# A two-layer transformer trunk: VectorE operands moved to PSUM, modulation products placed one by one, QKV weight splits on GpSimd

## Chip, cores and metric

One core of one Trainium2 chip. The metric is the device time of one execution in microseconds; the runs shown are medians of several executions.

## What is computed

1024 latent tokens and 256 context tokens of width 1024 pass two layers. Cut to what matters here:

```python
for i in range(DEPTH):
    ...
    hx = _modulate(_rms(x, norm_mix_g[i]), sx1, cx1)
    if i % 2 == 0:
        x = x + gx1 * _conv_fourier_mixer(hx, ab_w_in[j], ab_conv_w[j], ab_w_out[j])
        ...
    else:
        w = na_w_qkv[j]
        hc = _modulate(_rms(ctx, norm_mix_g[i]), sc1, cc1)
        q = _heads(hx, w[:, :hd], na_q_g[j])
        k = _heads(hx, w[:, hd:2 * hd], na_k_g[j])
        v = _heads(hx, w[:, 2 * hd:])
        ...
    x = x + gx2 * _mlp(_modulate(_rms(x, norm_mlp_g[i]), sx2, cx2), mlp_w1[i], mlp_w2[i])
    if not last:
        ctx = ctx + gc2 * _mlp(_modulate(_rms(ctx, norm_mlp_g[i]), sc2, cc2), mlp_w1[i], mlp_w2[i])
return x

def _mlp(h, w1, w2):
    return jnp.square(jax.nn.relu(h @ w1)) @ w2
```

The modulation (shift, scale and gate of each sublayer) is `cond_x @ ada_w[i] + ada_b[i]` for latent and the same with `cond_c` for context tokens.

Everything is fp32 accurate. The kernel gets there by splitting each operand into a rounded high part (fp32r) and a low part, low = value - high, and adding three matmuls: high x high, high x low, low x high.

## The kernel before, in words

Tokens lie in three chunks of columns: 0 and 1 with 512 latent tokens each, 2 with 256 context tokens. `xT[d][ci]` is the residual stream, 8 row tiles `d`. A bank is one of eight PSUM tiles of 128x512 (`bank()`); `tmp()` has four and `keep()` three SBUF tiles of that size. A weight tile is 128x512, two lie in a raw tile; raw tiles rotate through three buffers (tag `wraw`), split tiles through four (`wsp`). `split_act` (L251) makes a split: ScalarE (ACT) casts the high part (L252), the named engine subtracts for the low part (L253).

The program's stages: mixer of layer 0 (to 425 us), the context pass (425 to 664), the first MLP for latent tokens (664 to 1343), QKV (1343 to 1712), attention, second MLP.

**Context pass** (from L1268). The MLP of layer 0 on the 256 context tokens: 128 weight tiles, each with twelve matmuls of 128x256 (L299 to L301). `ctx_make` (L952) splits them, every third on VectorE (DVE), the others on GpSimd (POOL). In the up half, `dense` fills a bank; ACT takes ReLU and squares it twice, once as fp32r high part, and DVE subtracts (L1275 to L1278). In the down half `residual` (L316) adds the bank to `xT`. After each group `beside_step` runs one step of a list `beside0`: the norm that feeds the latent MLP (`Norm.stat` and `Norm.out`, chunks 1 and 0; odd row tiles multiply on POOL at L412, even ones on DVE at L405), then the token sums `sums_12` and `sum_3` (`whole` at L985 joins high and low part of a quarter, differences follow, `parts_of` splits them), and `sum_4`.

**First MLP** (`Seven`, L1013). Products of quarters are combined by sums, seven instead of eight, in 16 units. In a unit `head` and `tail` make the up half: sums from PSUM with `s1` (L1119, L1123, L1010), then `squared`; `down` makes 16 groups with a residual add each. Beside `down` run the products of the modulation for layer 1: `ada_step` (L216) takes one raw tile of `ada_w` and does eight multiply-and-accumulate operations (L223) in one go, twice per unit in units 0 to 13. The last unit's `down_by_chunk` has the squares (`Norm.square`, L378) and statistics (L388, a matmul with ones) of layer 1's first norm beside it.

**QKV** (from L1457): six units of 512 columns, each with 8 or 10 token tiles of 24 matmuls (L1466 to L1468). The norm's remaining outputs stand in the first unit (`later`); `load_qkv` splits four of the next unit's tiles early and four after its last tile; `tick` runs what was put off: transposes of normalised queries and keys (`turn`, L102) two or four tiles later, and `ada_filler`, eight products at a time.

Order of work: PE's instructions keep the program's order where `in_order` says so (L1168); everywhere else the scheduler orders each engine's queue by a simulated timeline when the program is built. SP issues the DMAs in its own order.

## Time and profile before

| | us |
|---|---|
| median of 3 runs | 2775.05 (2773.75 to 2775.78) |
| the profiled execution | 2776.96 |
| its span, first to last instruction | 2775.0 |
| TensorE (PE) busy | 2624.0 |
| VectorE (DVE) busy | 1952.0 |
| ScalarE (ACT) busy | 1041.8 |
| GpSimd (POOL) busy | 1236.3 |

Mean granted clock of TensorE 0.976. Busy time counts a matmul longer at the lower clock, so a stage's loss is idle time and clock together.

### The profile page before, as it was taken

To read this page: it belongs to the slowest core of one execution; us is meant where nothing else is said; L and a number is where in the kernel's file an instruction comes from. 1 tells how busy PE (TensorE), PEld (TensorE's weight loads), DVE (VectorE), ACT (ScalarE), POOL (GpSimd) and SP (SyncE) were. 2 spreads that over 40 slices of the span, in tenths; PEclk is the share of its full clock that TensorE was granted. 3 is DMA by queue.
4 is the path that set the end of the run, shared out by engine and by line. 5 is a ranking of instruction groups with operands and counts; after the bars stand their busy time and mean duration, and the time that the engine had idled before them with its cause. 6 is when DMAs were issued, how large, how long until landed. Compare 5 with 4: busy or idle time off the path is not lost. (4 is left out here: it accounts for less than half of the span.)

```text
span 2775.0 us, 38416 instructions
## 1 busy us (share of the span) xinstructions
PE 2624.0 (95%) x13883; PEld 2179.2 (79%) x13883; DVE 1952.0 (70%) x3986; ACT 1041.8 (38%) x2232; POOL 1236.3 (45%) x975
## 2 busy tenths in 40 slices
PE   7999898798999999999789999899999899999999
PEld 5888778797888888888667787688877688888887
DVE  5797679955776777775987453887879856556555
ACT  4211246554223223223432233666654323322322
POOL 3332347777445445445410011444447744544543
PEclk9999899999999999999999999899999999999999
DMA  7244324353222222222256344343411111111112
GB/s 249 67 139 130 119 62 129 111 171 122 84 73 88 82 71 84 82 74 77 80 167 184 117 131 152 115 152 107 139 50 39 42 43 61 54 49 50 61 46 84
DMA packets 170530, 273.08 MB, mean 98 GB/s; under 512 B 11308, under 2 KB 110924, under 8 KB 170084
## 3 DMA queue, kind: packets, MB, share of 16 engines
q1 hardware_dynamic: 168900, 268.01, 30.4%
q8 instruction: 109, 1.79, 0.3%
q10 hardware_dynamic: 1440, 2.62, 0.2%
q14 instruction: 81, 0.66, 0.1%
HBM read 241.21 MB, written 29.37 MB: 98 GB/s over the span
## 5 line engine op out<-in xcount | busy, mean ns | idle before, releaser
L253 POOL TENSOR_TENSOR wsp<-raw,wsp 128x512 fp32r<-128x512 f32 x454 | 644.3, 1424 | 782.7 <-ACT wsp L252 761.3
L316 DVE SCALAR_TENSOR_TENSOR xT<-ps,mods,xT 128x512 f32<-128x512 f32 (+1 forms) x672 | 470.5, 715 | 149.7 <-PE ps L301 148.9
L252 ACT CAST wsp<-raw 128x512 fp32r<-128x512 f32 x510 | 311.8, 618 | 648.2 <-PE ps L301 321.0
L223 DVE CUSTOM_DVE_ANT_0 junk<-raw,cond_b 128x256 bf16<-128x256 f32 x640 | 351.7, 550 | 106.2 <-DMA raw<-in_ada_t_dram 75.6
L1103 PE MATMUL ps<-mh,wsp 128*128 128x512 f32 (+1 forms) x1216 | 349.6, 368 | 8.1 <-DVE ny L1119 6.3
L1103 PEld LDWEIGHTS ps<-mh,wsp 128*128 128x128 f32 x1216 | 215.8, 189 | 49.3 <-ACT tmp L1003 4.4
L299 PE MATMUL ps<-uh,wsp 128*128 128x512 f32 x528 | 208.2, 394 | 8.8 <-DVE xT L316 6.7
L1103 PE MATMUL ps<-ml,wsp 128*128 128x512 f32 (+1 forms) x608 | 213.1, 368 | 0.0
L300 PE MATMUL ps<-ul,wsp 128*128 128x512 f32 x528 | 206.7, 391 | 1.2 <-DVE ul L1006 1.2
L301 PE MATMUL ps<-uh,wsp 128*128 128x512 f32 x528 | 206.6, 391 | 0.0
L301 PE MATMUL ps<-w,wsp 128*128 128x256 f32 (+1 forms) x512 | 172.4, 345 | 10.8 <-DVE wsp L253 8.6
L253 POOL TENSOR_TENSOR wsp<-tmp,wsp 128x512 fp32r<-128x512 f32 x60 | 81.4, 1356 | 224.5 <-ACT wsp L252 224.5
L300 PE MATMUL ps<-w,wsp 128*128 128x256 f32 (+1 forms) x512 | 173.6, 342 | 4.6 <-DVE w L1278 4.6
L299 PE MATMUL ps<-w,wsp 128*128 128x256 f32 (+1 forms) x512 | 173.1, 345 | 4.3 <-ACT wsp L252 3.0
L1010 DVE TENSOR_TENSOR tmp<-ps,ny 128x512 f32<-128x512 f32 x90 | 62.2, 691 | 126.4 <-PE ps L1103 124.4
L1005 POOL TENSOR_TENSOR tmp<-tmp 128x512 f32<-128x512 f32 x128 | 141.2, 1104 | 8.7 <-ACT uh L1004 6.7
L252 ACT CAST wsp<-tmp 128x512 fp32r<-128x512 f32 x60 | 37.3, 622 | 262.3 <-PE ps L301 257.6
L299 PE MATMUL ps<-hh,wsp 128*128 128x512 f32 (+1 forms) x360 | 130.4, 362 | 4.3 <-ACT wsp L252 3.9
L300 PE MATMUL ps<-hl,wsp 128*128 128x512 f32 (+1 forms) x360 | 129.5, 360 | 2.0 <-DVE hl L413 1.4
L301 PE MATMUL ps<-hh,wsp 128*128 128x512 f32 (+1 forms) x360 | 128.3, 357 | 1.5 <-POOL wsp L253 1.5
L299 PEld LDWEIGHTS ps<-uh,wsp 128*128 128x128 f32 x528 | 99.8, 189 | 35.8 <-DVE xT L316 7.3
L1103 PEld LDWEIGHTS ps<-ml,wsp 128*128 128x128 f32 x608 | 110.3, 189 | 17.8
(374 smaller groups left out, 6529.5 us busy)
## 6 DMA issues: line engine op xcount, KB each, us to landing
raw<-in_mlp_w_dram SPq DMA_DIRECT2D x192, 512.0 KB, 3.5
raw<-in_ada_t_dram SPq DMA_DIRECT2D x80, 512.0 KB, 3.5
...
```

Source lines behind the costliest of these rows:

```text
L223: DVE.tensor_tensor_reduce(out=junk, in0=raw[:, d * 256:d * 256 + 256], in1=cond_b, op0=ALU.mult, op1=ALU.add, scale=1.0, scalar=0.0, accu ...
L252: ACT.copy(dst_hi, src)
L253: lo_eng.tensor_tensor(out=dst_lo, in0=src, in1=dst_hi.bitcast(F32), op=ALU.subtract)
L299: PE.matmul(ps, lhsT=whi, rhs=ahi, start=first, stop=False)
L300: PE.matmul(ps, lhsT=whi, rhs=alo, start=False, stop=False)
L301: PE.matmul(ps, lhsT=wlo, rhs=ahi, start=False, stop=last)
L316: DVE.scalar_tensor_tensor(out=xT[dt][ci], in0=ps, scalar=mods[l][:, 24 * k + 16 + dt, s:s + 1], in1=xT[dt][ci], op0=ALU.mult, op1=ALU.add)
L1005: POOL.tensor_tensor(out=r, in0=r, in1=r, op=ALU.mult)
L1010: DVE.tensor_tensor(out=c, in0=ps, in1=s, op=ALU.add)
L1103: PE.matmul(ps[:, cs], lhsT=a, rhs=p, start=(first and kt == 0 and n == 0), stop=(kt == 3 and n == 2), skip_group_check=True)
```

## The change

What it does:

- The modulation products come one at a time (`ada_op`). In the first MLP two loads and two products per place in units 0 to 5, one of each in units 6 to 14; in QKV five products per token tile, in every tile from the second unit on and from the sixth tile of the first. Altogether 168 products are ordered into the first MLP (224 before) and 216 behind it (160 before).
- A `Norm` with `psum=(0, 1)` keeps its statistic `y` and each product `a` of chunks 0 and 1 in PSUM banks, and all its outputs go DVE, ACT, DVE. Both the context pass's norm and layer 1's first norm have it.
- `ctx_make`: every fourth weight tile is split by ACT, then ACT copies the high part to a bank and DVE subtracts from there; the other three go to POOL.
- Token sums: one `whole` on POOL, then `minus` twice on DVE into a bank.
- Context ReLU: DVE squares in the bank (max with 0, times r) in place of ACT.
- Last unit of the first MLP: the context squares stand in its tail, the context statistic right behind it.
- QKV: all splits on POOL.
- Second MLP: `sum_3` and `sum_4` in the new form, spread over two stages of eight places.

The diff, cut to what is spoken of:

```diff
--- before.py
+++ after.py
@@ -213,26 +213,38 @@
-    def ada_step():
...
-        l, m, kq, dh, raw = ada_raw.pop(0)
-        for s in range(2):
-            cond_b = ada_cond(kq, s)
-            for d in range(4):
-                DVE.tensor_tensor_reduce(out=junk, in0=raw[:, d * 256:d * 256 + 256], in1=cond_b, op0=ALU.mult,
-                                         op1=ALU.add, scale=1.0, scalar=0.0, accum_out=parts[:, kq, 4 * dh + d, s:s + 1])
...
+    def ada_op():
...
+        (l, m, kq, dh, raw), s, d = ada_open.pop(0)
+        cond_b = ada_cond(kq, s)
+        DVE.tensor_tensor_reduce(out=junk, in0=raw[:, d * 256:d * 256 + 256], in1=cond_b, op0=ALU.mult,
+                                 op1=ALU.add, scale=1.0, scalar=0.0, accum_out=parts[:, kq, 4 * dh + d, s:s + 1])
...
+    def ada_step():
+        for _ in range(8):
+            ada_op()
@@ -386,6 +402,13 @@
+            if ci in self.psum:
+                y, y0, t = bank()[:, :w], tmp()[:, :w], tmp()[:, :w]
+                self.y[ci] = y
+                return [lambda: ACT.activation(y0, ps[:, :w], AF.Abs_reciprocal_sqrt, scale=1.0 / D, bias=eps),
+                        lambda: DVE.scalar_tensor_tensor(out=t, in0=y0, scalar=-0.5 / D, in1=y0, op0=ALU.mult, op1=ALU.mult),
+                        lambda: DVE.scalar_tensor_tensor(out=t, in0=ps[:, :w], scalar=D * EPS, in1=t, op0=ALU.add, op1=ALU.mult),
+                        lambda: DVE.scalar_tensor_tensor(out=y, in0=t, scalar=1.5, in1=y0, op0=ALU.add, op1=ALU.mult)]
@@ -398,10 +421,10 @@
-            x, y, a = xT[dt][ci], self.y[ci], tmp()[:, :w]
+            x, y, a = xT[dt][ci], self.y[ci], (bank if ci in self.psum else tmp)()[:, :w]
-            if dt % 2 == 0 if on_dve is None else on_dve:
+            if ci in self.psum or (dt % 2 == 0 if on_dve is None else on_dve):
                 return (lambda: DVE.scalar_tensor_tensor(out=a, in0=x, scalar=g, in1=y, op0=ALU.mult, op1=ALU.mult),
...
@@ -857,7 +880,7 @@
-    norm = Norm(0, 1, m_hi, m_lo)
+    norm = Norm(0, 1, m_hi, m_lo, psum=(0, 1))
@@ -955,7 +978,14 @@
             w = wp.tile([P, 1024], F32R, tag="wsp", name="wsp")
-            split_act(w[:, 0:512], w[:, 512:1024], w_raw[n][:, 512 * k:512 * k + 512], DVE if w_at[0] % 3 == 1 else POOL)
+            raw = w_raw[n][:, 512 * k:512 * k + 512]
+            if w_at[0] % 4 == 1:
+                p = bank()
+                ACT.copy(w[:, 0:512], raw)
+                ACT.copy(p, w[:, 0:512].bitcast(F32))
+                DVE.tensor_tensor(out=w[:, 512:1024], in0=raw, in1=p, op=ALU.subtract)
+            else:
+                split_act(w[:, 0:512], w[:, 512:1024], raw, POOL)
@@ -1110,21 +1140,28 @@
             self.product(b, self.t["t2"], True)
+            step()
             DVE.tensor_tensor(out=u2, in0=b, in1=s1, op=ALU.add)
             self.product(a, self.quarter(upper, H0), False)
+            step()
             squared(tmp(), *part(0, H0), a)
             self.product(b, self.quarter(lower, H1), False)
...
             DVE.tensor_tensor(out=u3, in0=b, in1=s1, op=ALU.add)
             self.product(c, self.t["t1"], True)
+            step()
             c22 = added(c, u3)
             squared(c22, *part(1, H1), c22)
             self.product(b, self.t["t4"], False)
+            step()
...
@@ -1179,27 +1216,49 @@
+        def minus(self, p, b, t):
+
+            DVE.tensor_tensor(out=p, in0=b[0].bitcast(F32), in1=t, op=ALU.subtract)
+            DVE.tensor_tensor(out=p, in0=p, in1=b[1].bitcast(F32), op=ALU.add)
...
             def first():
-                f[0], f[1] = room(), room()
+                f[0] = room()
                 whole(b11, POOL, f[0])
-                whole(b12, DVE, f[1])
             def second():
-                f[2] = room()
-                whole(b22, POOL, f[2])
-                parts_of(t1, f[0], DVE)
+                f[1] = bank()
+                self.minus(f[1], b12, f[0])
 
             def third():
-                DVE.tensor_tensor(out=f[2], in0=f[2], in1=f[0], op=ALU.subtract)
+                parts_of(t1, f[1], DVE)
+
+            def fourth():
+                f[2] = bank()
+                ACT.copy(f[0], f[1])
+                self.minus(f[2], b22, f[0])
+
+            def fifth():
+                parts_of(t2, f[2], DVE)
                 self.t.setdefault("t1", []).append(t1)
                 self.t.setdefault("t2", []).append(t2)
 
-            return [first, lambda: DVE.tensor_tensor(out=f[0], in0=f[1], in1=f[0], op=ALU.subtract), second, third,
-                    lambda: parts_of(t2, f[2], DVE)]
+            return [first, second, third, fourth, fifth]
         def sum_3(self, kt, room=tmp):
...
+                f[0] = room()
+                whole(b12, POOL, f[0])
+
+            def second():
+                f[1] = bank()
+                self.minus(f[1], b22, f[0])
+
+            return [first, second, lambda: parts_of(b12, f[1], DVE)]
...
+            f2, p = room(), bank()
+            whole(self.t["t2"][kt], POOL, f2)
+            self.minus(p, self.quarter([kt + 4], H0)[0], f2)
+            parts_of(t4, p, DVE)
@@ -1230,10 +1291,12 @@
+        if (ci, which) == (2, 0):
+            return big("acc", F32)
...
-    norm1 = Norm(1, 0, a_hi, a_lo, room1)
+    norm1 = Norm(1, 0, a_hi, a_lo, room1, psum=(0, 1))
@@ -1270,11 +1333,10 @@
-            t = tmp()
-            r, q = t[:, 0:w2], t[:, w2:2 * w2]
-            ACT.activation(r, ps[:, :w2], AF.Relu)
+            r, q = tmp()[:, 0:w2], ps[:, :w2]
+            ACT.activation(r, q, AF.Relu)
             ACT.activation(uh[f][:, F0], r, AF.Square)
-            ACT.activation(q, r, AF.Square)
+            DVE.scalar_tensor_tensor(out=q, in0=q, scalar=0.0, in1=r, op0=ALU.max, op1=ALU.mult)
             DVE.tensor_tensor(out=ul[f][:, F0], in0=q, in1=uh[f][:, F0].bitcast(F32), op=ALU.subtract)
@@ -1305,8 +1367,14 @@
     def between0(i, us):
-        steps = [lambda: None] * 4 + [ada_issue, lambda: (ada_step(), ada_issue()), lambda: None, ada_step]
-        s0.down(us, None, steps if i < 14 else ())
+        def ada(n):
+            if ada_raw:
+                for _ in range(n):
+                    ada_op()
+
+        two = i < 6
+        s0.down(us, (lambda m, ci: (ada_issue() if (m, ci) == (4, 0) or two and (m, ci) == (4, 1) else None,
+                                    ada(2 if two else 1) if m > 3 and (m, ci) > (4, 0) else None)) if i < 15 else None)
@@ -1316,14 +1384,26 @@
-        todo = [[lambda d=d: norm1.square(d, 2) for d in range(4 * k, 4 * k + 4)] for k in range(2)]
-        todo += [[], [], [lambda: norm1.stat(2)]] + [[lambda d=d: norm1.out(d, 2, True) for d in (2 * k, 2 * k + 1)] for k in range(4)]
-        todo += [[], [], [], [], [lambda: norm1.stat(0)]] + [[lambda d=d: norm1.out(d, 0)] for d in range(2)]
-        s0.down_by_chunk(us, lambda m, ci: norm1.square(m, ci, POOL if m % 2 else DVE), todo)
-
+        norm1.stat(2)
+        todo = [[lambda d=d: norm1.out(d, 2, True) for d in (2 * k, 2 * k + 1)] for k in range(4)]
+        todo += [[] for _ in range(7)] + [[lambda: norm1.stat(0)]] + [[lambda d=d: norm1.out(d, 0)] for d in range(4)]
+        s0.down_by_chunk(us, lambda m, ci: norm1.square(m, ci, POOL if m % 2 and ci else DVE), todo)
+    s0.beside = [lambda: None] * 3 + [lambda k=k: [norm1.square(d, 2) for d in range(4 * k, 4 * k + 4)] for k in range(2)]
...
-    fillers.extend([ada_filler] * 21)
+    def ada_ops(n):
+        def run():
+            if not ada_raw and ada_next:
+                ada_issue()
+            if len(ada_raw) == 1 and ada_next:
+                ada_issue()
+            for _ in range(n):
+                ada_op()
+        return run
+
+    fillers.extend([ada_ops(5)] * (-(-8 * len(ada_next + ada_raw) // 5) + 1))
@@ -1338,7 +1418,7 @@
-            split_act(wt[:, 0:512], wt[:, 512:1024], raw, POOL if kt % 2 else DVE)
+            split_act(wt[:, 0:512], wt[:, 512:1024], raw, POOL)
@@ -1451,7 +1531,7 @@
-    later = {0: outs(0, 2, 5), 1: outs(0, 5, 8), 3: [lambda: norm1.stat(1)] + outs(1, 0, 2), 4: outs(1, 2, 5), 5: outs(1, 5, 8)}
+    later = {0: outs(0, 4, 6), 1: outs(0, 6, 8), 2: [lambda: norm1.stat(1)] + outs(1, 0, 1), 3: outs(1, 1, 3), 4: outs(1, 3, 5), 5: outs(1, 5, 8)}
@@ -1469,7 +1549,7 @@
-            tick(n == 2 or n < 5 and i > 3 and i % 2 == 0 or 0 < n < 5 and i % 2 == 0)
+            tick(n > 0 or i > 4)
@@ -1500,7 +1580,7 @@
-            qn = keep()
+            qn = x_all[2][:, 2 * (0, 2, 3)[i]:2 * (0, 2, 3)[i] + 2, :].rearrange("p a b -> p (a b)") if n == 0 and i < 3 else keep()
@@ -1516,7 +1596,7 @@
-            after(4 if n == 0 and i < 4 else 2, turn)
+            after(4 if n == 0 and i < 3 else 2, turn)
@@ -1685,8 +1765,7 @@
-        for f in s1.sums_12(kt, *(halves(op_.tile([P, NLAT], F32R, tag=g, name=g)) for g in ("oh", "ol"))):
-            f()
+        s1.sums_12_plain(kt, *(halves(op_.tile([P, NLAT], F32R, tag=g, name=g)) for g in ("oh", "ol")))
@@ -1712,8 +1791,9 @@
-    s1.down(us[:2], None, [lambda kt=kt: [f() for f in s1.sum_3(kt)] for kt in range(4)])
-    s1.down(us[2:], None, [lambda kt=kt: s1.sum_4(kt, halves(big("t4"))) for kt in range(4)])
+    steps = [f for kt in range(4) for f in s1.sum_3(kt)] + [lambda kt=kt: s1.sum_4(kt, halves(big("t4"))) for kt in range(4)]
+    s1.down(us[:2], None, steps[:8])
+    s1.down(us[2:], None, steps[8:])
```

How it moves the instructions, in three places.

POOL in the context pass (`ny`, `mh`, `ml`: a sum and the parts it comes from; `wsp`: split weights). Before:

```order
L985 TENSOR_TENSOR ny<-mh_2951,ml_2959 128x512
L253 TENSOR_TENSOR wsp<-raw,wsp 128x512 x2
L985 TENSOR_TENSOR ny<-mh_2948,ml_2956 128x512
L412 TENSOR_TENSOR tmp<-xT_84,ny 128x512
L253 TENSOR_TENSOR wsp<-raw,wsp 128x512
L985 TENSOR_TENSOR ny<-mh_2952,ml_2960 128x512
L253 TENSOR_TENSOR wsp<-raw,wsp 128x512 x3
L985 TENSOR_TENSOR ny<-mh_2949,ml_2957 128x512
```

Now:

```order
L265 TENSOR_TENSOR wsp<-raw,wsp 128x512 x21
L1015 TENSOR_TENSOR ny<-mh_2949,ml_2957 128x512
L265 TENSOR_TENSOR wsp<-raw,wsp 128x512
L1015 TENSOR_TENSOR ny<-mh_2950,ml_2958 128x512
L265 TENSOR_TENSOR wsp<-raw,wsp 128x512 x6
L1015 TENSOR_TENSOR ny<-mh_2951,ml_2959 128x512
L265 TENSOR_TENSOR wsp<-raw,wsp 128x512 x20
```

Norm multiplications (L412) are gone from there, the joins (L1015, before L985) are fewer, and splits stand in long runs.

DVE in the context pass (`w`: low half of the squared ReLU or a sum's part). Before:

```order
L985 TENSOR_TENSOR ny<-mh_2947,ml_2955 128x512
L253 TENSOR_TENSOR wsp<-raw,wsp 128x512
L1278 TENSOR_TENSOR w_3677<-tmp,w_3673 128x256
L1201 TENSOR_TENSOR ny<-ny 128x512
L253 TENSOR_TENSOR w_3677<-ny,w_3677 128x512
L1278 TENSOR_TENSOR w_3678<-tmp,w_3674 128x256
L1197 TENSOR_TENSOR ny<-ny 128x512
L253 TENSOR_TENSOR wsp<-raw,wsp 128x512
L413 TENSOR_TENSOR ml_2956<-tmp,mh_2948 128x512
L1278 TENSOR_TENSOR w_3679<-tmp,w_3675 128x256
```

Now:

```order
L986 TENSOR_TENSOR wsp<-raw,ps 128x512
L1222 TENSOR_TENSOR ps<-ps,ml_2957 128x512
L328 SCALAR_TENSOR_TENSOR xT_86<-ps,mods_75,xT_86 128x256
L265 TENSOR_TENSOR w_3681<-ps,w_3681 128x512
L328 SCALAR_TENSOR_TENSOR xT_86<-ps,mods_75,xT_86 128x256
L1221 TENSOR_TENSOR ps<-mh_2953,ny 128x512
L1222 TENSOR_TENSOR ps<-ps,ml_2961 128x512
L1339 SCALAR_TENSOR_TENSOR ps<-ps,tmp 128x256
L265 TENSOR_TENSOR w_3677<-ps,w_3677 128x512
L1340 TENSOR_TENSOR w_3681<-ps,w_3677 128x256
L986 TENSOR_TENSOR wsp<-raw,ps 128x512
```

Splits of weights (L986), the two steps of a sum (L1221, L1222) and the ReLU's two steps (L1339, L1340) each have one operand `ps`; before, the instructions of this piece had both in SBUF.

DVE in the last unit of the first MLP and behind it (`acc`: sum of the context's squares). Before, its tail and then the context statistic (L391) after latent and context squares (L378):

```order
L1119 TENSOR_TENSOR ny<-ps,ny 128x512
L1123 TENSOR_TENSOR ny<-ps,ny 128x512
L1006 TENSOR_TENSOR w_3680<-tmp,w_3679 128x512
L1010 TENSOR_TENSOR tmp<-ps,ny 128x512 x2
L1006 TENSOR_TENSOR ul<-tmp,uh 128x512
L1010 TENSOR_TENSOR tmp<-ps,ny 128x512
L1006 TENSOR_TENSOR ul<-tmp,uh 128x512
...
L378 TENSOR_TENSOR ny<-ny,tmp 128x256 x2
L378 TENSOR_TENSOR ny<-ny,tmp 128x512
L391 TENSOR_SCALAR tmp<-ps 128x256
L358 SCALAR_TENSOR_TENSOR tmp<-ny 128x256
```

Now:

```order
L1152 TENSOR_TENSOR ny<-ps,ny 128x512
L1158 TENSOR_TENSOR ny<-ps,ny 128x512
L1036 TENSOR_TENSOR w_3684<-tmp,w_3683 128x512
L394 TENSOR_TENSOR acc<-acc,tmp 128x256 x2
L1040 TENSOR_TENSOR tmp<-ps,ny 128x512
L394 TENSOR_TENSOR acc<-acc,tmp 128x256 x4
L1040 TENSOR_TENSOR tmp<-ps,ny 128x512
L394 TENSOR_TENSOR acc<-acc,tmp 128x256
L1036 TENSOR_TENSOR ul<-tmp,uh 128x512
L1040 TENSOR_TENSOR tmp<-ps,ny 128x512
L414 TENSOR_SCALAR tmp<-ps 128x256
```

The seven context additions (L394) stand between the tail's sums (L1040), and the statistic's first step (L414) before the tail's last low part.

## Rows read from the trace of the kernel before

**Rows 1.** The page, its first part: busy us (share) and instructions of an engine.
```profile
PE 2624.0 (95%) x13883; PEld 2179.2 (79%) x13883; DVE 1952.0 (70%) x3986; ACT 1041.8 (38%) x2232; POOL 1236.3 (45%) x975
```

**Rows 2.** Stages: length, busy us (instructions) of each engine, granted clock, DMA share, GB/s.
```profile
425.00:680.00 255.00, 219.37 (x1603) 205.71 (x1602) 194.32 (x224) 139.39 (x293) 187.51 (x128) 0.95 0.44 139
575.00:664.00 89.00, 81.72 (x650) 78.80 (x648) 51.37 (x77) 47.92 (x108) 59.31 (x43) 1.00 0.52 171
665.00:670.00 5.00, 4.37 (x11) 3.31 (x11) 0.00 (x0) 0.64 (x2) 4.48 (x4) 0.50 0.00 0
680.00:1300.00 620.00, 611.88 (x2934) 513.96 (x2933) 440.71 (x890) 178.04 (x295) 292.74 (x222) 1.00 0.25 80
1300.00:1425.00 125.00, 100.63 (x425) 78.04 (x424) 109.07 (x236) 59.41 (x109) 48.93 (x35) 0.92 0.30 91
1425.00:1560.00 135.00, 124.81 (x551) 101.40 (x550) 90.22 (x338) 35.27 (x71) 16.16 (x12) 0.96 0.61 184
```

**Rows 3.** Timeline of PE at 664 us: start, duration, instruction xcount [idle before].
```profile
664.13 1.07 PE L1103 MATMUL ps<-w,wsp 128*128 128x512 f32 x2 [3.95 <-ACT wsp L252]
```

**Rows 4.** PE's waits, 425 to 680 us: total us, times, longest.
```profile
PE ps L301 <- DVE wsp L253: 15.1, 13, 2.4
PE ps L301 <- POOL wsp L253: 6.9, 8, 1.8
PE ps L300 <- DVE w L1278: 4.6, 4, 1.5
```

**Rows 5.** DVE in the context pass by form: xcount | busy, mean ns | idle.
```profile
L253 DVE TENSOR_TENSOR wsp<-raw,wsp 128x512 fp32r<-128x512 f32 x42 | 45.9, 1094 | 12.6 <-ACT wsp L252 12.5
L1278 DVE TENSOR_TENSOR w<-tmp,w 128x256 fp32r<-128x256 f32 x32 | 31.9, 998 | 17.8 <-ACT tmp L1277 17.8
L316 DVE SCALAR_TENSOR_TENSOR xT<-ps,mods,xT 128x256 f32<-128x256 f32 x64 | 29.0, 477 | 15.7 <-PE ps L301 15.7
```

**Rows 6.** Timeline of DVE, 655 to 663 us.
```profile
661.42 0.41 DVE L253 TENSOR_TENSOR ml<-tmp,mh 128x256 fp32r<-128x256 f32 x1
661.75 0.68 DVE L1055 TENSOR_TENSOR raw<-raw 128x512 f32<-128x512 f32 x1
```

**Rows 7.** POOL in the context pass by form, and its timeline near 659 us.
```profile
L253 POOL TENSOR_TENSOR wsp<-raw,wsp 128x512 fp32r<-128x512 f32 x84 | 125.0, 1500 | 43.5 <-ACT wsp L252 40.2 <-issue 2.3 <-DVE tmp L405 0.6
...
659.67 1.28 POOL L1221 TENSOR_TENSOR tmp<-tmp 128x512 f32<-128x512 f32 x1 [0.69 <-DVE tmp L985]
```

**Rows 8.** ACT in the context pass by form.
```profile
L252 ACT CAST wsp<-raw 128x512 fp32r<-128x512 f32 x127 | 76.4, 615 | 49.2 <-PE ps L301 35.7 <-issue 4.7 <-DMA raw<-in_mlp_w_dram 3.6
```

**Rows 9.** The page's costliest groups.
```profile
L1010 DVE TENSOR_TENSOR tmp<-ps,ny 128x512 f32<-128x512 f32 x90 | 62.2, 691 | 126.4 <-PE ps L1103 124.4
```

**Rows 10.** Waits of PE, then of DVE, 680 to 1300 us.
```profile
PE ps L1103 <- DVE ny L1119: 6.3, 5, 1.6
...
DVE junk L223 <- DMA raw<-in_ada_t_dram: 22.8, 14, 1.7
```

**Rows 11.** PE's waits, 1300 to 1560 us.
```profile
PE ps L1467 <- DVE wsp L253: 8.0, 3, 5.0
PE ps L388 <- DVE ny L378: 5.5, 1, 5.5
PE ps L1468 <- DVE al L407: 4.9, 3, 2.8
PE ps L1468 <- DVE al L413: 4.7, 3, 2.0
PE ps L102 <- DVE ny L1504: 4.0, 4, 1.7
```

**Rows 12.** DVE's groups by form, 1343 to 1560 us.
```profile
L223 DVE CUSTOM_DVE_ANT_0 junk<-raw,cond_b 128x256 bf16<-128x256 f32 x160 | 75.0, 469 | 38.3 <-DMA raw<-in_ada_t_dram 32.0 <-DMA cond_b<-cond_d 2.6 <-issue 1.2
L1499 DVE TENSOR_REDUCE sm<-tmp 128x8 f32<-128x512 f32 x20 | 13.5, 677 | 4.3 <-ACT tmp L1496 4.3
L1514 DVE SCALAR_TENSOR_TENSOR tmp<-ps,qk_gain,tmp 128x512 fp32r<-128x512 f32 x18 | 13.4, 743 | 0.0
```

More of the change, by code (lines that the diff above doesn't have):

```diff
@@ L214, in ada_cond @@
         return in_cond[s][1]
-    def ada_step():
-        l, m, kq, dh, raw = ada_raw.pop(0)
-        for s in range(2):
-            cond_b = ada_cond(kq, s)
-            for d in range(4):
-                DVE.tensor_tensor_reduce(out=junk, in0=raw[:, d * 256:d * 256 + 256], in1=cond_b, op0=ALU.mult,
-                                         op1=ALU.add, scale=1.0, scalar=0.0, accum_out=parts[:, kq, 4 * dh + d, s:s + 1])
-            if ada_raw:
-                ada_cond(ada_raw[0][2], s)
+    ada_open = []
+    def ada_op():
+        if not ada_open:
+            if not ada_raw:
+                return
+            ada_open.extend((ada_raw[0], s, d) for s in range(2) for d in range(4))
+        (l, m, kq, dh, raw), s, d = ada_open.pop(0)
+        cond_b = ada_cond(kq, s)
+        DVE.tensor_tensor_reduce(out=junk, in0=raw[:, d * 256:d * 256 + 256], in1=cond_b, op0=ALU.mult,
+                                 op1=ALU.add, scale=1.0, scalar=0.0, accum_out=parts[:, kq, 4 * dh + d, s:s + 1])
+        if s == 1 and d == 3:
+            ada_raw.pop(0)
+        if d == 3:
+            nxt = ada_raw[1:] if s == 0 else ada_raw
+            if nxt:
+                ada_cond(nxt[0][2], s)
             elif ada_next:
                 ada_cond(ada_next[0][2], s)
-        if (kq, dh) == ada_last(m):
+        if (s, d) == (1, 3) and (kq, dh) == ada_last(m):
             mm = mods[l][:, 8 * m:8 * m + 8, :]
@@ L360, in rsqrt_newton, with __init__ @@
                 lambda: DVE.scalar_tensor_tensor(out=y, in0=t, scalar=1.5, in1=y, op0=ALU.add, op1=ALU.mult)]
+    eps = pp.tile([P, 1], F32, name="eps")
+    POOL.memset(eps, EPS)
     class Norm:
-        def __init__(self, l, k, hi, lo, room=None):
-            self.l, self.k, self.hi, self.lo = l, k, hi, lo
+        def __init__(self, l, k, hi, lo, room=None, psum=()):
+            self.l, self.k, self.hi, self.lo, self.psum = l, k, hi, lo, psum
             self.acc, self.y = {}, {}
@@ L1018, in __init__ @@
             self.l, self.hi, self.lo, self.units, self.room = l, hi, lo, units, room
-            self.t, self.raws, self.sums, self.made, self.makers = {}, {}, {}, [], []
+            self.t, self.raws, self.sums, self.made, self.makers, self.beside = {}, {}, {}, [], [], []
             add = self.makers.append
@@ L1111, in head, with tail @@
             return a, s1
-        def tail(self, i, head):
+        def tail(self, i, head, beside=()):
             a, s1 = head
+            beside = list(beside)
+            step = lambda: beside.pop(0)() if beside else None
             us = self.room(i)
@@ L1127, in tail @@
             self.product(b, self.t["t4"], False)
+            step()
             c21 = added(b, s1)
@@ L1170, in run @@
                 for i in self.units:
-                    us = self.tail(i, head)
+                    us = self.tail(i, head, self.beside if i + 1 not in self.units else ())
                     if i + 1 in self.units:
@@ L1209, in first, with sum_4 @@
             def first():
-                f[0], f[1] = room(), room()
-                whole(b12, DVE, f[0])
-                whole(b22, POOL, f[1])
-            return [first, lambda: POOL.tensor_tensor(out=f[0], in0=f[1], in1=f[0], op=ALU.subtract), lambda: parts_of(b12, f[0], DVE)]
-        def sum_4(self, kt, t4):
-            f21, f2 = tmp(), tmp()
-            whole(self.quarter([kt + 4], H0)[0], POOL, f21)
-            whole(self.t["t2"][kt], DVE, f2)
-            POOL.tensor_tensor(out=f21, in0=f21, in1=f2, op=ALU.subtract)
-            parts_of(t4, f21, DVE)
+                f[0] = room()
[4 more added lines that the diff above has]
+            return [first, second, lambda: parts_of(b12, f[1], DVE)]
+        def sum_4(self, kt, t4, room=tmp):
+            f2, p = room(), bank()
+            whole(self.t["t2"][kt], POOL, f2)
+            self.minus(p, self.quarter([kt + 4], H0)[0], f2)
+            parts_of(t4, p, DVE)
             self.t.setdefault("t4", []).append(t4)
```

10 lines of the change are left out of this document (added).

## The prediction

> **What bounds the kernel now.** I read the busy shares first, then a table of stages, then TensorE's waits in the stages that lose time, and last the single durations behind those waits.
>
> TensorE (PE) is busy for 2624.0 of the 2775.0 us [rows 1], so only stages where PE waits, or runs at a lower clock after a wait, can give time. I take a stage's loss as its length minus PE's busy time, plus its length times what the granted clock lacks of 1. The table gives [rows 2]:
> - context pass with the first split of the next stage (425 to 680 us): 255 - 219.4 = 35.6 idle and 0.05 x 255 = 12.8 of clock, 48.4 us.
> - first MLP's units (680 to 1300): 8.1 idle, clock 1.00.
> - end of the last unit and first QKV unit (1300 to 1425): 24.4 idle, 0.08 x 125 = 10.0 of clock, 34.4 us.
> - QKV up to 1560: 10.2 idle, 0.04 x 135 = 5.4 of clock, 15.6 us.
>
> [...]
>
> In the context pass PE waits 15.1 us for weight splits made by VectorE (DVE), 6.9 for those made by GpSimd (POOL) and 4.6 for the low half of the squared ReLU (DVE) [rows 4]. Those producers are slow there. A DVE split takes 1094 ns on average and a 128x256 subtraction 998 [rows 5]; with POOL idle, DVE takes 0.68 us for a 128x512 and 0.41 for a 128x256 subtraction of two SBUF inputs [rows 6]. POOL's split takes 1500 ns, a POOL subtraction of that size with less beside it 1.28 us [rows 7]. The residual add of the same stage, which reads PSUM, takes 477 ns [rows 5], though POOL is busy for 188 of 255 us [rows 2]. So I read: DVE operations with both inputs in SBUF and POOL operations lengthen each other; those with one input in PSUM are spared.
>
> **The change, part by part.**
>
> 1. Context pass. Of DVE's 42 splits and 32 subtractions, 42 x 0.41 + 32 x 0.59 = 36 us of busy time is lengthening [rows 5, 6]; of POOL's 84 splits it is 84 x 0.22 = 18 us [rows 7]. Now 32 splits go through a PSUM bank to DVE and 96 to POOL; the norm's outputs leave POOL, and most token sums move to DVE with one operand in PSUM. The order on POOL shows long unbroken runs of splits. Added is an ACT copy in every fourth tile, 32 x 0.62 = 20 us [rows 8]; ACT, busy for 139 of 255 us [rows 2], then stays below PE. What will be left I read from the stretch that is already calm: from 575 to 664 PE idles 7.3 of 89 us at clock 1.00 [rows 2], 3.95 of it in the wait that ends at 664.13 [rows 3]. The other 3.3 in 85 us make 8 over some 200 us; with the closing wait of 4 and its clock (half of some 6 us, 3) about 15 us remain. Gain 48.4 - 15 = 33. Lower end 10: half of the waits for DVE's work (15.1 + 4.6). Upper end 45: little but the closing wait remains.
>
> DVE also pays for reading PSUM: 477 ns for 256 columns [rows 5] against 0.41 us [rows 6], 691 ns for 512 [rows 9] against 0.68. Some 130 converted operations times 0.07 make at most 9 us of DVE time, off the path while DVE has slack. [...]
>
> 2. First MLP's units. PE's waits here are mainly five for the sum of PSUM and head, 6.3 us [rows 10]. DVE is late because products of the modulation stand ahead of that sum, and it waits 22.8 us in 14 stops for their weights [rows 10]. DVE's order keeps 16 products in each of the first six units and has 8 from the seventh on. Three of the five waits lie in what is kept. Gain two of five, 2.5, say 3; ends 0 and 6.
>
> 3. End of the last unit, first QKV unit. The context statistic costs a wait of 5.5 us [rows 11], and I put the same 3 us of clock to it as above. Its squares now stand in the unit's tail, between DVE's last sums, so its matmul finds them done: 9 us. If those seven additions (about 0.4 each) made the sums late, PE would wait 2.8 us once; seven PE products cover them. In the first QKV unit PE waits 9.6 us for low parts of the norm [rows 11]. The POOL multiplication drops out of half the outputs, and DVE's steps no longer collide. With clock and smaller waits 34.4 - 9 = 25 us are there; I take 9 of them. Sum 18; ends 4 (half of the statistic's share) and 28.
>
> 4. Other QKV units. DVE's splits cost 8.0 us of waits, 5.0 of it in one place [rows 11], where they stood behind products. With all splits on POOL this goes, with its clock. Against it: four POOL splits of 1.28 to 1.5 us in a row, 5 to 6 us, before the first four of eight weight tiles are whole, where two engines shared them. One tile of PE time about covers that, since casts start while the old unit's last tile runs. DVE gets 5 products a tile, 5 x 0.47 = 2.3 us and a short read of each sum, and for queries and keys three operations of 0.68 to 0.74 with small steps between [rows 12]: some 5 us, where the 24 matmuls of a tile take PE 24 x 124.8 / 551 = 5.4 us [rows 2], with transposes on top. It fits, not by much. SP's queue carries 27 instead of 20 modulation loads there, between weight loads, in the same three raw buffers: a late product holds a buffer, and the next weights behind it. Gain 8; ends -15 (a 2 us wait and 3 of clock at each of three boundaries) and 14.
>
> 5. Attention is not touched. In the second MLP sums change places in a stage with little DVE work: 0; ends -3 and 3.
>
> Sum: 33 + 3 + 18 + 8 = 62. The profiled execution took 2776.96 us, 1.9 over the median 2775.05; 2776.96 - 62 = 2715, and 2713 on the scale of the median.
>
> **Rivals.**
>
> A. The feeding chain bounds the context pass, not the collisions: a raw tile has three buffers and passes DMA, ACT, POOL or DVE. For: POOL has 96 splits instead of 84. Against: ACT's casts idle 49.2 us there, 35.7 of it behind PE and 3.6 behind DMA [rows 8]. Part 1 then gives 10: 2713 + 23 = 2736.
>
> B. DVE is full in QKV: 216 products instead of 160 from there on, each with two SBUF inputs, beside a POOL that makes every split. For: DVE already waits 32 us for the products' weights [rows 12]. Then normalised queries come late, PE waits at the transposes (4.0 us now [rows 11]), the clock falls: parts 3 and 4 give 9 and -10 instead of 18 and 8, so 2713 + 27 = 2740.
>
> C. The price of reading PSUM, all 9 us of it, lands on the path, because converted operations stand ahead of residual adds that PE waits for: 2722. The 512-column rows speak against it [rows 6, 9]. [...]
>
> D. Slower: the eight PSUM banks run out in the context pass. A norm's statistic, each output between its three steps, each DVE split and each sum now hold a bank; the up half's result stays until two DVE steps behind the ReLU are done. If PE waits w for a bank in each of its 32 + 64 groups, 96 w is lost. Above w = 62 / 96 = 0.65 us the change loses; w = 1 gives 2713 + 96 = 2809. Against: no wait for a bank is among PE's larger waits now [rows 4]. For: DVE works in order, and a late ACT step holds every bank queued behind it.
>
> **How the numbers follow.** Forecast 0.56, A 0.17, B 0.14, C 0.04, D 0.09. Within 0.2% (5.5 us, about what a measurement of this kernel can tell from no change) it lands only with D near its turning point: 0.03; slower, the rest of D: 0.06; faster 0.91. The range takes in A and B, and below the forecast the upper ends of part 1 and of part 3 or 4, not all at once: 2688 to 2752.
>
> **What would show it.** Right: a context pass of about 205 us instead of 239 up to the first split of the next stage, DVE's 128x256 subtraction there below 0.5 us and its 512-wide steps near 0.7, POOL's splits near 1.3, PE's waits for DVE's splits under 5 us in sum; no wait for the context statistic; no 5 us gap at the fourth QKV unit. Wrong: context pass over 215 us (A), transposes waiting over 10 us in sum (B), PE waiting in the context pass for residual adds or ReLU squares, which hold the banks (D).

## The result, and the profile after

The changed kernel took 2704.78 us (median of 4 runs, 2699.89 to 2712.83) against 2774.4 for the kernel before (median of 4); ratio 0.9752, 95% interval 0.9725 to 0.9778. Its profiled execution took 2701.67 us with a span of 2699.9, 75.3 us under the one of before. The forecast was 2713, range 2688 to 2752.

The profile after, stage by stage (columns as in [rows 2]; the stretches are those of [rows 2], shifted by what had been gained up to there):

```profile
425.00:640.00 215.00, 206.68 (x1614) 200.26 (x1614) 147.10 (x262) 141.43 (x286) 155.96 (x120) 0.99 0.52 165
640.00:1255.00 615.00, 612.11 (x2943) 515.94 (x2942) 416.41 (x778) 180.35 (x300) 291.68 (x223) 1.00 0.24 75
1255.00:1380.00 125.00, 102.61 (x444) 80.81 (x444) 112.94 (x259) 57.26 (x109) 45.68 (x34) 0.93 0.36 110
1380.00:1500.00 120.00, 116.04 (x518) 95.30 (x517) 74.22 (x295) 28.52 (x56) 20.55 (x16) 0.97 0.57 174
```

Both programs issue 13883 matmuls on PE. If n of them lie ahead of the same piece of work in both, the start of the n-th one marks the same place in both traces, wherever it lies in time. The numbers n were taken near the stages' edges: 7180 lies five token tiles into the second QKV unit, 7580 in the third tile of the fourth, 8200 two tiles before QKV's end. The forecasts are put to the stretch that holds the waits they speak of:

| stage | n from, to | before | after | difference | forecast |
|---|---|---|---|---|---|
| up to the context pass | 0, 2090 | 426.4 | 423.9 | -2.5 | 0 |
| context pass, first unit's start | 2090, 3660 | 250.9 | 208.5 | -42.4 | -33 |
| first MLP's units | 3660, 6661 | 631.1 | 624.6 | -6.5 | -3 |
| last unit's down half, first QKV unit | 6661, 7180 | 149.9 | 142.4 | -7.5 | -18 |
| second to fourth QKV unit | 7180, 7580 | 101.9 | 95.8 | -6.1 | -8 |
| next QKV units | 7580, 8200 | 132.9 | 133.3 | +0.4 | in the -8 |
| end of QKV, attention's start | 8200, 9000 | 120.4 | 111.9 | -8.5 | 0 |
| rest | 9000, 13882 | 955.6 | 953.6 | -2.0 | 0 |

So the sum of 62 was near the truth of 75 partly by luck, because misses cancel: two stages gave more than forecast, one less than half, and one that counted as untouched gave 8.5.

**Context pass.** PE's waits there now (total us, times, longest), against [rows 4]:

```profile
PE ps L313 <- POOL wsp L265: 3.9, 5, 1.0
PE ps L313 <- DVE wsp L986: 2.6, 2, 1.7
PE ps L1133 <- POOL wsp L265: 1.0, 1, 1.0
```

The groups of DVE and POOL by form (xcount | busy, mean ns), against [rows 5, 7]:

```profile
L328 DVE SCALAR_TENSOR_TENSOR xT<-ps,mods,xT 128x256 f32<-128x256 f32 x64 | 29.8, 477 | 9.1 <-PE ps L313 9.1
L986 DVE TENSOR_TENSOR wsp<-raw,ps 128x512 fp32r<-128x512 f32 x31 | 21.2, 683 | 4.7 <-ACT ps L985 4.2
L1339 DVE SCALAR_TENSOR_TENSOR ps<-ps,tmp 128x256 f32<-128x256 f32 x32 | 13.8, 430 | 27.5 <-ACT tmp L1337 27.2
L1340 DVE TENSOR_TENSOR w<-ps,w 128x256 fp32r<-128x256 f32 x32 | 13.5, 423 | 7.8 <-ACT w L1338 7.1
L1221 DVE TENSOR_TENSOR ps<-mh,ny 128x512 f32<-128x512 f32 x12 | 13.3, 1111 | 0.3 <-ACT ny L1241 0.3
L428 DVE SCALAR_TENSOR_TENSOR ps<-xT,g,ps 128x512 f32<-128x512 f32 x16 | 12.0, 749 | 0.1
```
```profile
L265 POOL TENSOR_TENSOR wsp<-raw,wsp 128x512 fp32r<-128x512 f32 x96 | 125.7, 1324 | 42.6 <-ACT wsp L264 39.5 <-PE ps L313 2.2 <-DVE xT L328 0.2
```

A split takes 683 ns where it took 1094, the ReLU's subtraction 423 instead of 998, POOL's split 1324 instead of 1500. The sum's first step (L1221), whose two inputs are still in SBUF, takes 1111. PE waits for DVE's splits 2.6 us instead of 15.1, and the granted clock is 0.99.

**First MLP and what follows.** PE's waits in the units, against [rows 10], then from the last unit into QKV, against [rows 11]:

```profile
PE ps L1133 <- DVE ny L1152: 2.1, 2, 1.1
```
```profile
PE ps L404 <- DVE ny L394: 11.4, 1, 11.4
PE ps L102 <- DVE ny L1584: 8.8, 2, 4.8
...
PE ps L404 <- DVE acc L394: 0.7, 1, 0.7
PE ps L1547 <- POOL wsp L265: 0.6, 1, 0.6
```

The context statistic waits 0.7 us instead of 5.5. In its place a single new wait of 11.4 us has appeared: the statistic of latent chunk 0 (L404) waits for the additions of its squares (L394). DVE's timeline before it (start, duration, instruction, no idle between):

```profile
1278.28 0.67 DVE L394 TENSOR_TENSOR ny<-ny,tmp 128x512 f32<-128x512 f32 x1
1278.88 1.51 DVE L430 SCALAR_TENSOR_TENSOR al<-tmp,mods,ah 128x256 fp32r<-128x256 f32 x1
1280.31 0.47 DVE L428 SCALAR_TENSOR_TENSOR tmp<-xT,g,ny 128x256 f32<-128x256 f32 x1
...
1283.48 1.55 DVE L394 TENSOR_TENSOR ny<-ny,tmp 128x512 f32<-128x512 f32 x1
1284.95 1.48 DVE L430 SCALAR_TENSOR_TENSOR al<-tmp,mods,ah 128x256 fp32r<-128x256 f32 x1
...
1287.77 3.15 DVE L394 TENSOR_TENSOR ny<-ny,tmp 128x512 f32<-128x512 f32 x3
1290.84 1.75 DVE L394 TENSOR_TENSOR xT<-xT,tmp 128x512 f32<-128x512 f32 x1
```

Additions stand between outputs of the context norm, and both lengthen beside POOL's splits (1283.21 to 1287.57 us): to 1.55 and 1.48 us, where the addition at 1278.28 took 0.67 and the low part at 1281.37, with POOL idle, 0.47.

### The profile page after: what moved, and what is told of

Same layout as the page of the kernel before. It is cut to its first block, busy times and chain, and to the rows that moved or that the text cites. A ratio compares the mean times of both kernels' runs of the same rounds, so it can differ in the third digit from the quotient of the medians.

```text
span 2699.9 us, 38461 instructions
## 1 busy us (share of the span) xinstructions
PE 2598.2 (96%) x13883; PEld 2169.2 (80%) x13883; DVE 1886.1 (70%) x4019; ACT 1039.3 (38%) x2220; POOL 1202.1 (45%) x971
## 4 chain that ended last, share of the span: by engine, by line
PE 70%; DVE 11%; DMA 4%; issue 3%; POOL 1%; ACT 1%; SPq 0%; DVEq 0%; ACTq 0%; POOLq 0%
PE ps L1133 20%; PE ps L311 11%; PE ps L312 11%; PE ps L313 11%; PE ps L1684 3%; PE ps L102 3%; PE ps L1547 3%; PE ps L1548 3%; PE ps L1546 3%; DVE junk L227 2%; DMA raw<-in_ada_t_dram 2%; PE ps L1499 2%; DVE xT L328 1%; PE ps L1501 1%; DVE ny L394 1%
## 5 line engine op out<-in xcount | busy, mean ns | idle before, releaser
L265 POOL TENSOR_TENSOR wsp<-raw,wsp 128x512 fp32r<-128x512 f32 x477 | 655.8, 1381 | 819.2 <-ACT wsp L264 797.1
L264 ACT CAST wsp<-raw 128x512 fp32r<-128x512 f32 x478 | 293.5, 620 | 607.2 <-PE ps L313 308.1
L227 DVE CUSTOM_DVE_ANT_0 junk<-raw,cond_b 128x256 bf16<-128x256 f32 x640 | 336.7, 526 | 123.4 <-DMA raw<-in_ada_t_dram 95.5
L1133 PE MATMUL ps<-mh,wsp 128*128 128x512 f32 (+1 forms) x1216 | 348.2, 367 | 2.9 <-DVE ny L1152 2.1
L1133 PEld LDWEIGHTS ps<-mh,wsp 128*128 128x128 f32 x1216 | 215.5, 189 | 41.7 <-ACT tmp L1033 4.1
L1133 PE MATMUL ps<-ml,wsp 128*128 128x512 f32 (+1 forms) x608 | 212.7, 367 | 0.0
L1040 DVE TENSOR_TENSOR tmp<-ps,ny 128x512 f32<-128x512 f32 x90 | 62.2, 691 | 114.4 <-PE ps L1133 112.2
L1133 PEld LDWEIGHTS ps<-ml,wsp 128*128 128x128 f32 x608 | 110.1, 189 | 17.9
```

Of the source, the lines that this page charges most:

```text
L227: DVE.tensor_tensor_reduce(out=junk, in0=raw[:, d * 256:d * 256 + 256], in1=cond_b, op0=ALU.mult, op1=ALU.add, scale=1.0, scalar=0.0, accu ...
L264: ACT.copy(dst_hi, src)
L265: lo_eng.tensor_tensor(out=dst_lo, in0=src, in1=dst_hi.bitcast(F32), op=ALU.subtract)
L1133: PE.matmul(ps[:, cs], lhsT=a, rhs=p, start=(first and kt == 0 and n == 0), stop=(kt == 3 and n == 2), skip_group_check=True)
```

## Experiments

Each was timed beside the kernel before on its chip. The stage times below come from the matmul numbers of the table above; where an edit does not touch a stage, it took 207.4 to 208.7 us (context pass), 621.8 to 626.5 (first MLP's units), 142.2 to 143.4 (last unit's down half, first QKV unit) and 93.8 to 96.4 (second to fourth QKV unit). The first 2090 matmuls, in a stretch that no edit touches, took 423.9 to 428.4 us in the thirteen traces of the changed kernel and its variants, and the kernel before took 2774.4 to 2778.9 us beside them. Totals are therefore compared to some 4 us, and the argument rests on stage times.

**1. Where the operand lies (context pass).**

```diff
-                p = bank()
+                p = tmp()
...
-            r, q = tmp()[:, 0:w2], ps[:, :w2]
+            t = tmp()
+            r, q = t[:, 0:w2], t[:, w2:2 * w2]
...
-            DVE.scalar_tensor_tensor(out=q, in0=q, scalar=0.0, in1=r, op0=ALU.max, op1=ALU.mult)
+            DVE.scalar_tensor_tensor(out=q, in0=ps[:, :w2], scalar=0.0, in1=r, op0=ALU.max, op1=ALU.mult)
```

> The changed kernel with two operands of the context pass back in SBUF: the copied high part of every fourth split, and the square that the ReLU's subtraction reads; same engines, same number of operations. Theory P (an operand in PSUM spares DVE and POOL each other): DVE's split goes from 683 to 950 ns or more, the ReLU subtraction from 423 to 700 or more, POOL's split from 1324 towards 1400, and the context pass takes 5 to 20 us longer. Rival F (the changed mix of engines and the freed POOL feed the pass, the place of the operand does not matter): durations may change, but the pass stays within 3 us.

Measured: 2717.41 us; the context pass took 219.8 us instead of 208.5, 11.3 longer. DVE's and POOL's groups there:

```profile
L986 DVE TENSOR_TENSOR wsp<-raw,tmp 128x512 fp32r<-128x512 f32 x32 | 33.9, 1060 | 1.9 <-ACT tmp L985 1.2
...
L1341 DVE TENSOR_TENSOR w<-tmp,w 128x256 fp32r<-128x256 f32 x32 | 24.4, 765 | 6.7 <-ACT w L1339 5.8
```
```profile
L265 POOL TENSOR_TENSOR wsp<-raw,wsp 128x512 fp32r<-128x512 f32 x97 | 138.5, 1448 | 40.6 <-ACT wsp L264 37.9 <-PE ps L313 2.2
```

With the same operations on the same engines, the place of one operand makes a split 1060 instead of 683 ns, the subtraction 765 instead of 423, POOL's split 1448 instead of 1324. Theory P holds; F, which had the pass within 3 us, falls for this part.

**2. The old norm, and the old splits, in the context pass.**

```diff
-    norm = Norm(0, 1, m_hi, m_lo, psum=(0, 1))
+    norm = Norm(0, 1, m_hi, m_lo)
```

> The changed kernel with the context pass's norm as before (statistic and products in SBUF, odd outputs over POOL), all else changed. Theory P: 16 outputs collide with POOL again, DVE's steps of the norm go from 0.75 to 1.1 us or more and POOL gets 8 multiplications; the pass takes 3 to 12 us longer. Rival F (feeding): within 2 us.

```diff
-            if w_at[0] % 4 == 1:
+            if w_at[0] % 3 == 1:
+                split_act(w[:, 0:512], w[:, 512:1024], raw, DVE)
+            elif False:
```

> The changed kernel with the context pass's splits as before: every third by DVE from SBUF, two thirds by POOL, no second ACT copy. Theory P: 43 splits of about 1.05 us instead of 31 of 0.68, 24 us more DVE work, POOL's 85 at 1.4; the pass takes 8 to 20 us longer, near the 11 us of the run with SBUF operands or above. Rival F (POOL's share feeds the pass): POOL has fewer splits, so within 3 us or shorter.

Measured: pass 213.4 us (+4.9, total 2709.85) with the old norm, 213.7 (+5.2, total 2711.94) with the old splits, the latter under what was expected. The norm's product and, in the other kernel, the split:

```profile
L428 DVE SCALAR_TENSOR_TENSOR tmp<-xT,g,ny 128x512 f32<-128x512 f32 x8 | 11.7, 1480 | 0.0
```
```profile
L265 DVE TENSOR_TENSOR wsp<-raw,wsp 128x512 fp32r<-128x512 f32 x42 | 40.7, 968 | 9.0 <-ACT wsp L264 8.4
```

In the changed kernel the product took 749 ns. Undone alone, each part costs 5 to 11 us; the whole was 42. DVE's busy time in the pass rose by 26 us in experiment 1, by 9 and by 19 here (144.6 in the changed kernel, 190.5 before), so my reading is that DVE has slack once the other parts are in place, and most of one part's lengthening is covered. No run here undid all of them at once: that the mechanism acts is shown, but at least half of the 42 us is put to it by argument, and what POOL's shorter work gave (busy 151 instead of 185 us) is not separated.

**3. The new wait of 11.4 us.** Statistic two groups later (its four outputs then at two places instead of four), odd rows' squares on POOL as before, and both:

```diff
-        todo += [[] for _ in range(7)] + [[lambda: norm1.stat(0)]] + [[lambda d=d: norm1.out(d, 0)] for d in range(4)]
+        todo += [[] for _ in range(9)] + [[lambda: norm1.stat(0)]] + [[lambda d=d: norm1.out(d, 0) for d in (2 * k, 2 * k + 1)] for k in range(2)]
-        s0.down_by_chunk(us, lambda m, ci: norm1.square(m, ci, POOL if m % 2 and ci else DVE), todo)
+        s0.down_by_chunk(us, lambda m, ci: norm1.square(m, ci, POOL if m % 2 else DVE), todo)
```

> The changed kernel with the statistic of latent chunk 0 two groups later in the last unit of the first MLP (where it stood before the change). Theory Q (DVE's queue: the seven additions of squares stand behind the context outputs, and the statistic's matmul waits 11.4 us for them): two groups are 2.7 us of PE work, so the wait falls by 3 to 5 us and the total by 2 to 5. Rival G (given back: DVE is the bound from the tail to the middle of the first QKV unit, so PE waits the same time later): wait falls as much, total within 2 us of the changed kernel's 2705.

> The changed kernel with the odd rows' squares of chunk 0 added on POOL again, place unchanged. Theory Q: four of seven additions leave DVE, some 4 to 6 us of its queue, so the 11.4 us wait falls to 5 to 8 and the total by 4 to 7. Rival G: total within 2 us of 2705. If POOL, busy with splits of QKV weights, is the late one instead, the wait stays near 11.

> Both: statistic two groups later and odd squares on POOL. Theory Q: wait below 4 us, total 8 to 14 us below the changed kernel, near 2693. Rival G: under 3 us of total gained, because the norm's outputs come late in the first QKV unit.

The wait, in this order:

```profile
PE ps L404 <- DVE ny L394: 11.3, 1, 11.3
```
```profile
PE ps L404 <- POOL ny L394: 10.3, 1, 10.3
```
```profile
PE ps L404 <- POOL ny L394: 8.9, 1, 8.9
...
PE ps L1546 <- DVE tmp L410: 3.5, 1, 3.5
```

Totals 2708.52, 2703.26 and 2707.83; the stretch from the last unit's down half through the first QKV unit 142.1, 140.4 and 144.8 us instead of 142.4. Theory Q's sizes fail: with the statistic two groups later the scheduler ordered DVE's queue anew, and the additions ended 2.5 us later too, counted from the start of the stretch; where POOL had them, POOL was late; and with both edits PE waited 5.7 us in the first QKV unit at L1546 (3.5 of them in the row above), 1.7 in the changed kernel. Rival G had also expected the wait to fall, which it did not, but it fits in the length of the stretch: neither place nor engine of the additions makes it shorter by more than 2 us.

**4. Less work for DVE in that stretch.** Context outputs of layer 1's norm in PSUM, with their statistic; then, apart from it, no products in the first QKV unit:

```diff
-    norm1 = Norm(1, 0, a_hi, a_lo, room1, psum=(0, 1))
+    norm1 = Norm(1, 0, a_hi, a_lo, room1, psum=(0, 1, 2))
```

> The changed kernel with the context chunk's norm outputs of layer 1 in PSUM as well. Theory G: 8 products and 8 low parts of DVE stop colliding with POOL's splits (they took 0.47 to 1.5 us), 3 to 5 us less DVE work, so the 11.4 us wait for the statistic falls by 3 to 5 and the total by as much. Rival (banks run out, or only additions of two SBUF tiles matter): no gain, or a loss by waits for banks.

```diff
-            tick(n > 0 or i > 4)
+            tick(n > 0)
```

> The changed kernel without products in the first QKV unit (25 of them, 12 us of DVE, move behind it). Theory G (from the last unit's tail to the middle of the first QKV unit the whole of DVE's work sets the time, wherever the statistic stands): if the products lie inside that stretch, the wait at the transposes near 1344 us (4.8) goes and the stretch is 4 to 8 us shorter, some of it given back later. Rival (the stretch is over by the sixth tile, and the wait there comes from the order of the small steps): within 2 us.

Context outputs in PSUM: 2699.75 us (2697.89 to 2702.34, ratio to before 0.9727, interval 0.9691 to 0.9763). The wait and DVE's low parts, then those of the changed kernel:

```profile
PE ps L404 <- DVE ny L394: 4.9, 1, 4.9
```

```profile
L430 DVE SCALAR_TENSOR_TENSOR al<-ps,mods,ah 128x256 fp32r<-128x256 f32 x8 | 3.6, 482 | 0.0
```

```profile
L430 DVE SCALAR_TENSOR_TENSOR al<-tmp,mods,ah 128x256 fp32r<-128x256 f32 x8 | 6.6, 820 | 0.0
```

The low part falls from 820 to 482 ns, the wait from 11.4 to 4.9, the stretch from 142.4 to 138.5 us. This is the fastest version run; its interval overlaps that of the changed kernel, so 5 us stands on the stage times rather than on the totals.

No products in the first QKV unit: the stretch fell to 133.8 us, 8.6 shorter (PE's wait at the transposes there went from 4.8 to 0.7), but the total rose to 2717.84. The 25 products came at the end (84 products instead of 64 in the next QKV units, 16 instead of none in attention's start): the next QKV units took 144.6 instead of 133.3, with a wait of 8.6 us at the fourth unit's first transposes, and attention's start 126.8 instead of 111.9, where PE now waited for DVE:

```profile
PE ps L1499 <- DVE mx L1510: 8.8, 1, 8.8
```

So DVE's work bounds the stretch, as G says. The stretch, and DVE's busy time in it (us):

| kernel | stretch | DVE busy |
|---|---|---|
| before | 149.9 | 132.1 |
| changed | 142.4 | 125.1 |
| context outputs in PSUM | 138.5 | 118.9 |
| no products in the first QKV unit | 133.8 | 113.4 |
| both, products moved to the first MLP (next run) | 130.9 | 106.1 |

DVE's work is not alone in this: with additions on POOL (experiment 3) DVE was busy for 120.8 and 121.4 us, but the stretch took 140.4 and 144.8, because PE then waited for POOL. To gain from less DVE work, the products need a place with room. I tried the first MLP:

```diff
-    norm1 = Norm(1, 0, a_hi, a_lo, room1, psum=(0, 1))
+    norm1 = Norm(1, 0, a_hi, a_lo, room1, psum=(0, 1, 2))
-        two = i < 6
+        two = i < 9
-            tick(n > 0 or i > 4)
+            tick(n > 0)
```

> The changed kernel with three alterations: context outputs of layer 1's norm in PSUM, two raw tiles of products per unit up to the ninth unit of the first MLP instead of the sixth (192 products there, none in the first QKV unit). Theory G with room in the first MLP: first QKV unit 7 to 9 us shorter as in the run without products there, nothing lost at the end, 1 to 3 us of stalls in the three units; total 2690 to 2695. Rival (the products cost the same wherever they stand): 2700.

Measured: 2705.97 (ratio to before 0.9740; the changed kernel's 0.9752). The first QKV unit and the stretch ahead gained 11.5 us (130.9), but the first MLP took 629.6 instead of 624.6, its old waits back:

```profile
PE ps L1133 <- DVE ny L1152: 5.2, 4, 1.6
```

The later QKV units lost 8.1 (141.4), all of it at one place: matmuls 7580 to 7640, in the fourth unit, took 20.7 us instead of 12.6. The wait there, the longest of four from 1255 to 1800 us, shows why:

```profile
PE ps L102 <- DVE ny L1584: 10.3, 4, 5.1
```

The fourth unit's first transposes wait for keys that DVE normalises (L1584) behind and between products; the granted clock is 0.95 from 1480 to 1550 us, where the changed kernel has 1.00. The run without products in the first unit waited 8.6 us at the same place, the changed kernel 0.3. So the rival was nearer in the total, but not by a price that products have everywhere: what was gained in one place was lost where a product stood in front of something that PE needs next.

**5. QKV's other units.** Splits alternating again, products in bursts again, and both:

```diff
-            split_act(wt[:, 0:512], wt[:, 512:1024], raw, POOL)
+            split_act(wt[:, 0:512], wt[:, 512:1024], raw, POOL if kt % 2 else DVE)
...
-    fillers.extend([ada_ops(5)] * (-(-8 * len(ada_next + ada_raw) // 5) + 1))
+    fillers.extend([ada_filler] * 30)
...
-            tick(n > 0 or i > 4)
+            tick(n == 2 or n < 5 and i > 3 and i % 2 == 0 or 0 < n < 5 and i % 2 == 0)
```

> The changed kernel with the QKV weight splits alternating between DVE and POOL again. If DVE's splits queued behind products were what stalled the unit boundaries (8.0 us of PE's waits before), the stretch between the first QKV unit and the fourth gets 5 to 10 us longer and waits for DVE splits come back. Rival (the pacing of the products, five per tile, removes the stall by itself): that stretch stays within 2 us, waits for splits under 2 us.

> The changed kernel with QKV's products in bursts of eight at the old places; splits all on POOL. If pacing matters by itself, queries and keys come late behind bursts and behind loads: PE's waits at transposes rise from 8.8 to 12 or more and the total by 3 to 8 us. Rival (splits on POOL are the whole gain there): within 2 us of the changed kernel, or faster, since fewer products stand in the first two units.

> The changed kernel with QKV's products in bursts and its splits alternating again. If either alone suffices against the stalls between the second and fourth QKV unit, that stretch goes from 95 to 99 us or more here, waits for DVE splits are back at 5 us or more. If neither is the cause (the order of the first unit's leftovers is), it stays at 95 to 97.

The second to fourth unit (matmuls 7180 to 7580) took 94.4, 96.6 and 102.0 us; before 101.9, changed 95.8. PE's waits for DVE's splits there with the first edit and with both (with bursts alone POOL makes all splits, and PE waits 0.6 us for them):

```profile
PE ps L1547 <- DVE wsp L265: 3.0, 2, 2.1
```

```profile
PE ps L1547 <- DVE wsp L265: 7.9, 2, 5.1
```

Either part alone takes the stall of 5 us at the splits away; only with both undone is it back. DVE's splits are harmless when products come one by one (94.4 us against 95.8). Bursts are not harmless when POOL splits: the stretch only ends three matmuls too early to show it. With bursts PE waits 11.1 us at matmul 7583, the fourth unit's first transposes, with both edits 3.7, in the changed kernel 0.3. All waits of this kind with bursts, 1255 to 1660 us (9.1, 3, 4.8 in the changed kernel), and DVE's timeline there:

```profile
PE ps L102 <- DVE ny L1584: 16.5, 4, 11.1
```
```profile
1505.42 1.37 DVE L227 CUSTOM_DVE_ANT_0 junk<-raw,cond_b 128x256 bf16<-128x256 f32 x1 [6.88 <-DMA raw<-in_ada_t_dram]
...
1510.93 0.68 DVE L1579 TENSOR_REDUCE sm<-tmp 128x8 f32<-128x512 f32 x1
...
1512.69 0.69 DVE L1584 TENSOR_TENSOR ny<-ps,sm 128x512 f32<-128x512 f32 x1
```

DVE stands 6.9 us for a burst's weights, does its eight products, and only then normalises the keys that the transposes need. The next units took 147.6 and 139.5 us instead of 133.3, with fewer products in them (40 and 36 instead of 64). The rest of the totals, 2731.10 and 2728.71, comes from attention's start (123.8 and 123.9 us): the old places hold fewer products than are left here, and eight ran that late. So the waits at the transposes rose as the pacing theory says, and the rival (splits on POOL are the whole gain) fails; the 3 to 8 us that the theory gave were too few: the next units alone lost 14.3 with bursts.

## Why the prediction was right, and where its steps failed

1. Context pass, 33 forecast, 42.4 measured, within its ends (10 and 45). The mechanism is shown by experiments 1 and 2, its whole size is not. Two terms were mis-sized. Of the 15 us left over, the closing wait of 4 us and its clock (3) were kept; the wait was 1.0 us (at L1133), with the clock at 0.99. And the loss counted was too small: over the 1570 matmuls of this stage PE's idle time fell by 27 us (35.5 to 8.3), where 24 were taken, but its busy time by 15 (215.5 to 200.2), where the clock term gave 10; what more than the clock shortened the matmuls is open. Rivals A and D did not happen: the pass took 208.5 us, and none of PE's waits that the profile lists there is for a bank. C has little room: 8.3 us of idle time and 0.01 x 215 of clock are all that the pass still loses. Its price was read from two different operations: the 477 ns are the residual add's, and it still takes 477. The ReLU's 256-column steps with an operand in PSUM take 423 to 430 ns (rows above, 0.41 from SBUF), the split 683 (0.68 from SBUF). That is some 20 ns at most, where the prediction counted 70 for each. That a removed wait gives its clock back, which the terms for clock take for granted, was an estimate that no run shows by itself. What the traces show: behind the closing wait of 3.95 us the next ten matmuls of 128x512 took 4.63 us (granted clock 0.50 from 665 to 670 us), behind the wait of 1.0 us now 2.60 (1.00 from 623 to 626 us), and over the pass the clock rose from 0.95 to 0.99.
2. First MLP, 3 forecast, 6.5 measured, just above the end of 6. I carried three of the five waits over because the order is unchanged; two came back, 2.1 us instead of 6.3. The other 2.3 us are within the spread of this stage. The run with 16 products in nine units (5.2 us of waits) suggests that these waits hang on the number per unit.
3. Last unit and first QKV unit, 18 forecast, 7.5 measured. The step "its matmul finds them done: 9 us" was right for the context statistic (0.7 us) and wrong as a sum: I did not follow what its additions and outputs push back on DVE. The 9.6 us of waits for low parts, from which the other 9 us were taken, went as forecast as well. But the statistic of chunk 0, two groups earlier and with its additions on DVE, now waits 11.4 us, and the transposes 6.0 instead of 2.3: PE's waits in this stretch sum to 22 us after and 25 before. The step that failed is to count a removed wait as gained without asking what DVE does next. Experiments 3 and 4 show the bound: DVE's work in the stretch, which fell only from 132.1 to 125.1 us. Neither the place nor the engine of those additions shortens it much, but sparing their neighbours the lengthening does (3.9 us).
4. Other QKV units, 8 forecast, 5.7 measured. The reason given, splits on POOL, is not the whole: for the stall at the splits, products one by one would have done it as well, and with splits on POOL alone the bursts stall the transposes instead (experiment 5). The feared POOL lateness was 0.6 us. Rival B came in part: up to 1650 us PE waits 9.1 us at transposes for normalised queries and keys and 1.2 us more for a norm step (L428), just over the 10 us that were its sign, but nothing like its price.
5. "Attention is not touched" failed as a statement on time: its start became 8.5 us shorter. The code is the same, but in the traces the instructions of all engines stand in another order there: the scheduler ordered the queues anew. PE's waits there before, and after:

```profile
PE ps L102 <- DVE p L1451: 12.6, 4, 5.4
PE ps L102 <- POOL p L1451: 3.1, 1, 3.1
```

```profile
PE ps L102 <- DVE p L1531: 7.8, 4, 3.5
```

Which reordered instruction does it was not tried; all variants without products left over had 111.9 to 115.7 us there. The 2.5 us at the program's head are within the spread named above.
